# Three edits to the hand-ordered stages of a hybrid streaming layer: the place of the sink column, the engine of the weight splits, and the prices by which the order is made

## The chip, the cores and the metric

The kernel runs on one core of a Trainium2 chip. The metric is the device time of one execution in microseconds (us). The kernel before takes 1554.15 us, the median of three runs that lie between 1549.72 and 1560.18 us.

The engines of the core are named as the profile names them: PE is TensorE (matmuls and transposes; PEld is its weight load), DVE is VectorE, ACT is ScalarE, POOL is GpSimd, SP is SyncE, which only issues DMAs here. Each engine works through its own queue in the order in which the instructions were written.

## The reference, cut to what matters

One layer for 2048 prompt tokens and 32 sample tokens (2080 columns), model width 1024, in float32:

```
h = rmsnorm(x);  z = h @ W_in        # split into q, k, v, gate_a, B, C, u, gate_c, merge_a, merge_c
q, k = rope(rmsnorm(q)), rope(rmsnorm(k))                # 8 q heads, 2 kv heads, head_dim 64
# attention: each chunk of 64 frames sees itself and the two chunks before it
m = maximum(max(s), sink);  e = exp(s - m);  p = e / (sum(e) + exp(sink - m))
y_a = ((p @ v) * silu(gate_a)) @ W_attn_out
y_c = (B * conv3(C * u) * silu(gate_c)) @ W_conv_out
r   = x + (sigmoid(merge_a) * y_a + sigmoid(merge_c) * y_c) @ W_o
out = r + sigmoid(r @ W_ple_gate) * (p_in @ W_ple_proj)
```

The learned sink of a head is one more score in each row of the softmax, with no value behind it.

## The kernel before, in words

**Precision.** A float32 operand is made into two parts: a high part, rounded by a copy on ACT, and a low part, which is the operand less the high part, by one subtraction. A product is then three matmuls: high by high, high by low, low by high. So each weight tile of 128x512 costs a copy on ACT and a subtraction, and each row of activations does too.

**Stages.** Large matrix products are made in Strassen's way with seven products of half size (numbers 1 to 7 in the code). The program has three stages.

1. A first phase (lines 842 to 1166): the rows of the first half of the tokens are normalised and split while PE fills the time with the small product with W_ple_proj (`product0`), and then runs the first products of `z` (`step0`, the first entries of the list `steps`). It ends at about 85 us.
2. The bulk of `z`, whose instructions are ordered by the framework, up to about 860 us. Its weight splits are lines 206 to 208, high part on ACT and low part on DVE. The change does not touch it.
3. From line 1225 on, the attention and all products after it: `yB` (W_conv_out), `pp` (W_ple_proj), `yA` (W_attn_out), and the products `b` of W_o and W_ple_gate in two passes (s=0 and s=1, over the first and the second half of the columns). It runs from about 860 us to the end. PE works through a fixed list of units (`run_units`, `run_big`), and the 17 attention tiles (`attention`) are begun at set amounts of PE work and dropped in between the matmuls of the units.

**What sets the order.** In stages 1 and 3 the order of the instructions on every engine is written by a small plan that runs while the kernel is built. Each engine call goes through `Engine.__getattr__` (line 119), which adds the price of the instruction (`cost`, line 101) to the clock of its engine: `now` for PE, `busy["V"]` for DVE, `busy["S"]` for ACT, `busy["G"]` for POOL, `busy["Y"]` for SP. Pieces of work are Python generators. `yield {}` means: go on once what I issued has ended by the plan, and 0.15 us for the semaphore have passed; `yield {"ps": 2}` also waits until two PSUM banks are free. After each matmul `due()` issues whatever the plan says is ready. So a price decides in which place of an engine's queue an instruction stands. On the chip the instructions then wait on semaphores, each engine in that order. All such instructions have line 136 in the profile (`return f(**kw)`), so they are told apart by the names of their tiles.

**Prices before.** A DVE operation of n elements per partition costs 0.13 + 0.0011 n us (0.3 for 16 or fewer), an ACT operation 0.2 + 0.00082 n, a POOL operation 0.35 + 0.0021 n, and its end is where the engine's clock then stands.

**The weight splits of stage 3** (`split_w`, line 1884). A weight tile `wr` is loaded by SP; ACT writes the high part into `w`; the low part is made by POOL for all tiles of the list before the first one of the second pass (`last_split`, line 1895), and by DVE from there on. Five `w` tiles exist.

**Attention of one chunk** (`sink_attention`, line 1230). For each of two kv heads a PSUM bank `S` is taken. ACT first copies the sink into one more column of the bank (line 1235), then PE writes the scores, two matmuls (KH and KL) for each of two groups (lines 1238 and 1239). DVE takes the row maximum `nm` over scores and sink; ACT makes `E` = exp with its sum; DVE inverts the sum `se`; ACT scales into `P`; PE transposes into `PT`; ACT and DVE split it into `pth` and `ptl`; PE multiplies with V into `O`; DVE multiplies with the gate into `at`. Before that, `attention` transposes, normalises and rotates q and k; `qs`, `KH` and `KL` are the split operands of the scores, written by ACT (high) and DVE (low). For `ss` POOL raises to the power -0.5.

Tiles named below: `xb_h`, `xb_l` are split rows of the products `b`; `c` are their results; `tk`, `tb` rows of the merge gates; `acf`, `ac_l` rows of the gated attention; `kn`, `qr` normalised heads.

Of the kernel before, what the change touches and what calls it, by code (L numbers as in the profile page):

```python
# [7 lines left out]
F32 = mybir.dt.float32  # L8
# [34 lines left out]
def tile_hybrid_stream_step(ctx: ExitStack, tc: tile.TileContext, x, xT, pT, wu, consts, rope, ckT, cv_dup,  # L43
                            ck_raw, cv_raw, yT, kpo, vpo, cpo, kso, vso, cso):
    nc = tc.nc
    add, sub, mul = ALU.add, ALU.subtract, ALU.mult
# [10 lines left out]
    def bank(name):  # L57
        return psp.tile([P, 512], F32, tag="ps", name=name)
# [28 lines left out]
    now, fin, seq, events = [0.0], [0.0], [0], []  # L87
    busy = {"V": 0.0, "S": 0.0, "G": 0.0, "Y": 0.0}
# [6 lines left out]
    def size(ap):  # L95
        n = 1
        for d in ap.shape[1:]:
            n *= d
        return n

    def cost(key, op, kw):
        if op == "dma_start":
            return 0.9 if kw.get("accum_op") is not None else 0.57 if key == "G" else 0.42
        n = size(kw["out"])
        if key == "T":
            return max(0.109, 0.00044 * n + 0.0064)
        if key == "S":
            return 0.2 + 0.00082 * n + (0.13 if kw.get("accum_out") is not None else 0.0)
        if key == "G":
            return 2.03 if kw.get("op") == ALU.pow else 0.35 + 0.0021 * n  # L110
        if op == "tensor_reduce":
            return 0.08 + 0.0012 * size(kw["in_"])
        return 0.3 if n <= 16 else 0.13 + 0.0011 * n

    class Engine:
        def __init__(self, key, engine):
# [2 lines left out]
        def __getattr__(self, op):  # L119
            f = getattr(self.engine, op)  # L120

            def call(**kw):
                us = cost(self.key, op, kw)
                if self.key == "T":
                    now[0] += us
                    end = now[0]
                else:
                    busy[self.key] = end = max(busy[self.key], now[0]) + us
                if op == "dma_start":
                    if wire[0] is None:  # L130
                        end += 6.6 if kw.get("accum_op") is not None else 5.2
                    else:
                        o = kw["out"]
                        wire[0] = end = max(end + 1.7, wire[0]) + o.shape[0] * size(o) * 4 / 390e3
                fin[0] = max(fin[0], end)
                return f(**kw)  # L136
            return call

    eV, eS, eG, eT, eY = [Engine(*x) for x in (("V", nc.vector), ("S", nc.scalar), ("G", nc.gpsimd), ("T", nc.tensor),
                                           ("Y", nc.sync))]  # L140
# [5 lines left out]
    def free(tag, n=1):  # L146
        live[tag] -= n
        assert live[tag] >= 0, tag
# [72 lines left out]
    G = len(groups)  # L221
# [78 lines left out]
    def tile_of(gs, q):  # L300
        return "AB GF DE C".split().index(next(x for x in "AB GF DE C".split() if q in x)) if len(gs) == 2 else q == "C"

    worder = []
    for s in steps:
        for s_ in s:
            key = ("s", *s_) if len(s_) == 3 else ("l", *s_[1:3], tile_of(s_[1], s_[3]))
            if key not in worder:
                worder.append(key)
    for kind, b, n, *p in plan:
        key = {"B": (kind, b, n, *p), "yB": ("q", 0, UY + n, 1), "pp": ("pp", b, n // 2),  # L310
               "yA": ("q", b, UY + n, 0)}[kind]
        key = ("pp", 2, n // 2) if kind == "pp" else key
# [181 lines left out]
    def norm(v, k, rb, q):  # L494
        nc.vector.scalar_tensor_tensor(out=v, in0=v, scalar=lng_sb[:, k:k + 1], in1=rb[:, :q], op0=mul, op1=mul)
# [8 lines left out]
    B, T = {}, {}  # L504
# [725 lines left out]
    def sink_attention(name, ng, lhs, krhs, cn, e_out, norm, keys, sk, done, last, lag):  # L1230
        GG = 2 * ng
        SS = []
        for kv in range(2):
            s = bank(f"S_{name}_{kv}").rearrange("p (g c) -> p g c", g=2)
            eS.copy(out=s[:, :ng, cn:cn + 1], in_=sk[:, kv * ng:(kv + 1) * ng].unsqueeze(2))
            kh, kl = krhs(kv)
            for j in range(ng):
                eT.matmul(out=s[:, j, :cn], lhsT=lhs(kv, j), rhs=kh, start=True, stop=False)
                eT.matmul(out=s[:, j, :cn], lhsT=lhs(kv, j), rhs=kl, start=False, stop=True)
            SS.append(s)  # L1240
        if last:
            free("qs")
        yield {}
        nmax = sm.tile([P, 4], F32, tag="nmax", name=f"nm_{name}")
        for kv in range(2):
            eV.tensor_reduce(out=nmax[:, kv * ng:(kv + 1) * ng], in_=SS[kv][:, :ng, :cn + 1],
                            axis=AX.X, op=ALU.max, negate=True)
        yield {}
        se = sm.tile([P, 4], F32, tag="se", name=f"se_{name}")
        for kv in range(2):  # L1250
            for j in range(ng):
                g = kv * ng + j
                eS.activation(out=e_out(kv, j), in_=SS[kv][:, j, :cn + 1], func=AF.Exp, bias=nmax[:, g:g + 1],
                              accum_out=se[:, g:g + 1])
            yield None
            yield None
        yield {}
        free("ps", 2)
        eV.reciprocal(out=se[:, :GG], in_=se[:, :GG])
        yield {}  # L1260
        for kv in range(2):
            for j in range(ng):
                g = kv * ng + j
                for src, dst in norm(kv, j):
                    eS.activation(out=dst, in_=src, func=AF.Copy, scale=se[:, g:g + 1])
            if kv == 0:
                yield None
        fin[0] += lag
        yield {"ps": 2, "ph": 1}
        w = ng * P  # L1270
        pts, parts = [], []
        for q0 in range(0, len(keys), 512 // w):
            qs = keys[q0:q0 + 512 // w]
            pp = bank(f"PT_{name}_{q0}")
            for i, (ins, kp_, vh, vl) in enumerate(qs):
                for j, src in enumerate(ins):
                    eT.transpose(out=pp[:kp_, i * w + j * P:i * w + (j + 1) * P], in_=src, identity=ident)
            cols = 256 if q0 else 512
            ph = sm.tile([P, cols], F32R, tag=f"pth{cols}", name=f"pth_{name}_{q0}", bufs=2)
            pl = sm.tile([P, cols], F32R, tag=f"ptl{cols}", name=f"ptl_{name}_{q0}", bufs=2)  # L1280
            i = 0
            while i < len(qs):
                e = i
                while e < len(qs) and qs[e][1] == qs[i][1]:
                    e += 1
                n = qs[i][1]
                parts.append((ph[:n, i * w:e * w], pl[:n, i * w:e * w], pp[:n, i * w:e * w]))
                i = e
            pts += [(ph[:n, i * w:(i + 1) * w], pl[:n, i * w:(i + 1) * w], vh[:n], vl[:n])
                    for i, (_, n, vh, vl) in enumerate(qs)]  # L1290
        yield {}
        free("P")
        for h, _, src in parts:
            eS.copy(out=h, in_=src)
        yield {}
        for x, (h, lo, src) in enumerate(parts):
            if x:
                yield None
            eV.tensor_tensor(out=lo, in0=src, in1=h.bitcast(F32), op=sub)
        yield {"ps": -1}  # L1300
        O = bank(f"O_{name}")
        for i, (ph, pl, vh, vl) in enumerate(pts):
            eT.matmul(out=O[:, :w], lhsT=vh, rhs=ph, start=(i == 0), stop=False)
            eT.matmul(out=O[:, :w], lhsT=vl, rhs=ph, start=False, stop=False)
            eT.matmul(out=O[:, :w], lhsT=vh, rhs=pl, start=False, stop=(i == len(pts) - 1))
        yield {}
        free("ph")
        done(O)
        yield {}
        free("ps")  # L1310
        if last:
            last()
# [571 lines left out]
    def split_w(i):  # L1884
        w = wp.tile([P, 2, 4, P], F32R, tag="w", name=f"w{i}")
        W2[i] = h, lo = w[:, 0], w[:, 1]
        src = raw_of.pop(i)
        eS.copy(out=h, in_=src)
        yield {}
        (eG if i < last_split else eV).tensor_tensor(out=lo, in0=src, in1=h.bitcast(F32), op=sub)  # L1890
        yield {}
        w_ready[i] = now[0]
        room["wf"] += 1

    last_split = next(i for i, key in enumerate(worder) if key[:2] == ("B", 1))
    x_at, load_at = [0], [0]
    LEAD, LOOK = 2, 11

    def next_loads():
# [33 lines left out]
        while n_split[0] < len(worder) and room["w"] > 0:  # L1933
            i = n_split[0]
            if landed.get(i, 1e9) > now[0] or busy["S"] >= now[0] + (0.3 if i > used[0] + 2 else 1.5):
                break
            room["w"] -= 1
            go(split_w(i))
            n_split[0] += 1
# [165 lines left out]
```

## Time and profile before

| | |
|---|---|
| runs of the kernel before | 1554.15 us median, 1549.72 to 1560.18 |
| the profiled execution | 1554.51 us, its span 1552.7 us |
| busy in the span: PE, DVE, ACT, POOL | 1504.6, 1219.8, 816.9, 491.6 us |
| mean granted PE clock | 0.990 |

The profile is of one execution. The 1.8 us between its own time and its span lie around the first and the last instruction. A row of "windows" gives a stretch from:to in us, its length, and then for PE, PEld, DVE, ACT and POOL the busy time with the number of instructions, the PE clock that was granted as a share of full speed, the share of DMA time, and GB/s. A row of "waits" reads: engine, tile and line that waited, the arrow, what ended the wait, then the total in us, the number of waits, and the longest. A row of the "timeline" is the start in us, the duration, engine, line, operation, out<-in, shape, how many of them in a row, and in brackets the idle time of the engine just before it with what ended it. A row of "groups" gives operation, tiles, shape and count, then total busy us and mean ns of one.

### The profile page before, as it was taken

What the parts mean: (1) busy time and instruction counts of PE and PEld (TensorE: products, weight loads), DVE (VectorE), ACT (ScalarE), POOL (GpSimd) and SP (SyncE); (2) the same over time, 40 slices, a digit from 0 to 9 for tenths busy, and PEclk for the clock granted to TensorE, in tenths of its full rate; (3) what the DMA queues carried; (4) which work ended last, traced back from release to release, by engine and by line L of the source; (5) the groups of instructions that cost most, each with busy time, mean ns of one, the idle gap of its engine ahead of it and who ended that gap; (6) DMA issues with size and microseconds to landing.
All of it is one profiled execution on the core that took longest, in us unless ns stands there. A gap on an engine that the chain in (4) does not pass through costs nothing. (4 is left out here: it accounts for less than half of the span.)

```text
span 1552.7 us, 28012 instructions
## 1 busy us (share of the span) xinstructions
PE 1504.6 (97%) x9553; PEld 1358.6 (87%) x9553; DVE 1219.8 (79%) x2242; ACT 816.9 (53%) x1933; POOL 491.6 (32%) x622
## 2 busy tenths in 40 slices
PE   9999999999999999999999999999988997999998
PEld 7878888888899999999999899887877886999998
DVE  7887878875689777899757678857799899569777
ACT  8453353344467544344556356775755676444453
POOL 2133322232212332344212222236647455410201
PEclk9999999999999999999999999999999999999999
DMA  9489886898778845344647766567847659995959
GB/s 336 156 295 341 312 301 211 270 348 274 248 255 276 284 160 159 118 135 133 196 162 251 246 221 202 185 184 222 195 122 197 155 170 270 256 266 143 256 146 279
DMA packets 199230, 346.88 MB, mean 223 GB/s; under 512 B 23728, under 2 KB 57072, under 8 KB 199088
## 3 DMA queue, kind: packets, MB, share of 16 engines
q1 hardware_dynamic: 157008, 239.42, 48.2%
q0 software_dynamic: 32432, 87.85, 19.8%
q10 hardware_dynamic: 9648, 17.83, 3.1%
q8 instruction: 75, 1.23, 0.3%
q14 instruction: 67, 0.55, 0.1%
HBM read 227.66 MB, written 117.46 MB: 222 GB/s over the span
## 5 line engine op out<-in xcount | busy, mean ns | idle before, releaser
L136 PE MATMUL b<-xb_h,w 128*128 128x264 f32 (+1 forms) x1344 | 314.2, 325 | 0.0
L136 PEld LDWEIGHTS b<-xb_h,w 128*128 128x128 f32 x1344 | 225.5, 190 | 19.0
L591 PE MATMUL a<-x_l,w 128*128 128x264 f32 (+1 forms) x744 | 228.1, 320 | 0.0
L589 PE MATMUL a<-x_h,w 128*128 128x264 f32 (+1 forms) x744 | 227.2, 320 | 0.1
L136 PE MATMUL b<-xb_l,w 128*128 128x264 f32 (+1 forms) x672 | 218.1, 325 | 0.0
L594 PE MATMUL a<-x_h,w 128*128 128x264 f32 (+1 forms) x744 | 201.5, 320 | 0.0
L207 ACT CAST w<-wr 128x512 fp32r<-128x512 f32 (+1 forms) x180 | 110.1, 618 | 105.2 <-PE c L594 34.5
L208 DVE TENSOR_TENSOR w<-wr,w 128x512 fp32r<-128x512 f32 (+1 forms) x180 | 136.6, 769 | 34.4 <-ACT w L207 34.0
L136 POOL TENSOR_TENSOR w<-wr,w 128x512 fp32r<-128x512 f32 x88 | 127.0, 1495 | 110.5 <-ACT w L136 96.1
L136 ACT CAST w<-wr 128x512 fp32r<-128x512 f32 x168 | 102.5, 620 | 106.1 <-PE b L136 31.5
L589 PEld LDWEIGHTS a<-x_h,w 128*128 128x128 f32 x744 | 139.9, 188 | 10.8 <-DVE s L795 0.3
L591 PEld LDWEIGHTS a<-x_l,w 128*128 128x128 f32 x744 | 139.7, 188 | 10.7
L136 PEld LDWEIGHTS b<-xb_l,w 128*128 128x128 f32 x672 | 127.8, 190 | 9.5
L594 PEld LDWEIGHTS a<-x_h,w 128*128 128x128 f32 x744 | 125.0, 188 | 10.5
L727 PE MATMUL la<-x_h,w 128*128 128x264 f32 x516 | 111.7, 285 | 1.2 <-ACT w L207 1.2
L589 PE MATMUL c<-x_h,w 128*128 128x512 f32 (+1 forms) x336 | 110.6, 340 | 0.0
L591 PE MATMUL c<-x_l,w 128*128 128x512 f32 (+1 forms) x336 | 110.7, 339 | 0.0
L207 ACT CAST w<-a 128x512 fp32r<-128x512 f32 x82 | 49.7, 621 | 98.2 <-DVE a L338 31.8
L594 PE MATMUL c<-x_h,w 128*128 128x512 f32 (+1 forms) x336 | 100.4, 340 | 0.0
L788 DVE SCALAR_TENSOR_TENSOR u<-u,c 128x264 f32<-128x264 f32 (+1 forms) x125 | 59.4, 507 | 44.8 <-ACT u L783 29.8
L136 PE MATMUL yB<-ycs_h,w 128*128 128x264 f32 (+1 forms) x384 | 91.0, 326 | 0.0
L136 PE MATMUL yA<-ac_h,w 128*128 128x264 f32 (+1 forms) x384 | 90.5, 325 | 0.0
(436 smaller groups left out, 3949.0 us busy)
## 6 DMA issues: line engine op xcount, KB each, us to landing
wr<-in_wu SPq DMA_DIRECT2D x177, 256.0 KB, 4.0
a<-in_wu SPq DMA_DIRECT2D x116, 256.0 KB, 5.2
wr<-ws SPq DMA_DIRECT2D x74, 256.0 KB, 3.5
wr<-qs SPq DMA_DIRECT2D x64, 256.0 KB, 4.1
ws<-a POOLq DMA_DIRECT2D x63, 256.0 KB, 4.0
qs<-a POOLq DMA_DIRECT2D x24, 256.0 KB, 5.7
z_s<-s2n POOLq DMA_DIRECT2D x21, 264.0 KB, 4.2
s<-z_s SPq DMA_DIRECT2D x21, 264.0 KB, 5.0
```

Of the source, the lines that this page charges most:

```text
L136: return f(**kw)
L207: nc.scalar.copy(out=hi, in_=src)
L208: nc.vector.tensor_tensor(out=lo, in0=src, in1=hi.bitcast(F32), op=sub)
L589: nc.tensor.matmul(out=ps[:, :cn], lhsT=w[:, 0, k], rhs=x[0][:, c0:c0 + cn], start=first and k == 0, stop=False, skip_group_check=True)
L591: nc.tensor.matmul(out=ps[:, :cn], lhsT=w[:, 0, k], rhs=x[1][:, c0:c0 + cn], start=False, stop=False, skip_group_check=True)
L594: nc.tensor.matmul(out=ps[:, :cn], lhsT=w[:, 1, k], rhs=x[0][:, c0:c0 + cn], start=False, stop=k == 3, skip_group_check=True)
L727: nc.tensor.matmul(out=ps[:, :m], lhsT=w[:, a, k], rhs=r[:, cols], start=q in "ABG" and j == 0 and e == 0, stop=j == 1 and e == 2, skip_gr ...
L788: nc.vector.scalar_tensor_tensor(out=t[:, c0:c0 + cn], in0=t[:, c0:c0 + cn], scalar=-1.0, in1=ps[:, :cn], op0=mul, op1=sub)
```

## The change

There are three edits.

- The prices of `cost` are set anew. A DVE operation costs 0.045 + 0.0011 n (0.09 for 16 or fewer), an ACT operation 0.1 + 0.00082 n, reductions 0.01 + 0.0012 n. A new table `LATE` is added to the end of an operation, though not to its engine's clock: so the time from one instruction to the next on an engine (the pitch) and the time at which a result is there are told apart. A POOL operation that is not a DMA now also moves DVE's clock, by 0.35 of its price (`BESIDE`). PE's prices move by about 1%. Both hand-ordered stages use these prices, so also the first steps of the first phase.
- In `sink_attention` the copy of the sink column stands after the score matmuls of both banks, with a `yield {}` between them, and another before the maximum.
- In `split_w` all low parts are made by DVE; `last_split` is gone.

No DMA, no matmul and no arithmetic is added or taken away. The diff in full:

```diff
--- before.py
+++ after.py
@@ -98,19 +98,22 @@
             n *= d
         return n
 
+    LATE = {"V": 0.08, "S": 0.1, "G": 0.25, "Y": 0.0}
+    BESIDE = [0.35]
+
     def cost(key, op, kw):
         if op == "dma_start":
-            return 0.9 if kw.get("accum_op") is not None else 0.57 if key == "G" else 0.42
+            return 0.6 if key == "G" else 0.42
         n = size(kw["out"])
         if key == "T":
-            return max(0.109, 0.00044 * n + 0.0064)
+            return max(0.1085, 0.000446 * n + 0.0028)
         if key == "S":
-            return 0.2 + 0.00082 * n + (0.13 if kw.get("accum_out") is not None else 0.0)
+            return 0.1 + 0.00082 * n + (0.13 if kw.get("accum_out") is not None else 0.0)
         if key == "G":
             return 2.03 if kw.get("op") == ALU.pow else 0.35 + 0.0021 * n
         if op == "tensor_reduce":
-            return 0.08 + 0.0012 * size(kw["in_"])
-        return 0.3 if n <= 16 else 0.13 + 0.0011 * n
+            return 0.01 + 0.0012 * size(kw["in_"])
+        return 0.09 if n <= 16 else 0.045 + 0.0011 * n
 
     class Engine:
         def __init__(self, key, engine):
@@ -125,7 +128,10 @@
                     now[0] += us
                     end = now[0]
                 else:
-                    busy[self.key] = end = max(busy[self.key], now[0]) + us
+                    busy[self.key] = max(busy[self.key], now[0]) + us
+                    end = busy[self.key] + LATE[self.key]
+                    if self.key == "G" and op != "dma_start":
+                        busy["V"] = max(busy["V"], now[0]) + BESIDE[0] * us
                 if op == "dma_start":
                     if wire[0] is None:
                         end += 6.6 if kw.get("accum_op") is not None else 5.2
@@ -1232,7 +1238,6 @@
         SS = []
         for kv in range(2):
             s = bank(f"S_{name}_{kv}").rearrange("p (g c) -> p g c", g=2)
-            eS.copy(out=s[:, :ng, cn:cn + 1], in_=sk[:, kv * ng:(kv + 1) * ng].unsqueeze(2))
             kh, kl = krhs(kv)
             for j in range(ng):
                 eT.matmul(out=s[:, j, :cn], lhsT=lhs(kv, j), rhs=kh, start=True, stop=False)
@@ -1240,6 +1245,9 @@
             SS.append(s)
         if last:
             free("qs")
+        yield {}
+        for kv in range(2):
+            eS.copy(out=SS[kv][:, :ng, cn:cn + 1], in_=sk[:, kv * ng:(kv + 1) * ng].unsqueeze(2))
         yield {}
         nmax = sm.tile([P, 4], F32, tag="nmax", name=f"nm_{name}")
         for kv in range(2):
@@ -1887,12 +1895,11 @@
         src = raw_of.pop(i)
         eS.copy(out=h, in_=src)
         yield {}
-        (eG if i < last_split else eV).tensor_tensor(out=lo, in0=src, in1=h.bitcast(F32), op=sub)
+        eV.tensor_tensor(out=lo, in0=src, in1=h.bitcast(F32), op=sub)
         yield {}
         w_ready[i] = now[0]
         room["wf"] += 1
 
-    last_split = next(i for i, key in enumerate(worder) if key[:2] == ("B", 1))
     x_at, load_at = [0], [0]
     LEAD, LOOK = 2, 11
 
```

## The prediction, as put on record before the changed kernel was run

> **What bounds the kernel now.** I read the page first, then the busy time by stretch, then who PE waits for, then single stretches of the timeline.
>
> ```profile
> span 1552.7 us, 28012 instructions
> ```
>
> The profiled execution took 1554.51 us, 1.8 more than this span, and lies 0.4 above the median of the runs shown, so sums made against it hold for the median too. By stretch:
>
> ```profile
> 0.00:85.00 85.00, 81.71 (x350) 64.71 (x351) 68.89 (x116) 53.05 (x96) 18.49 (x38) 1.00 0.67 243
> 85.00:860.00 775.00, 771.73 (x4903) 699.82 (x4902) 606.81 (x1118) 368.60 (x757) 224.31 (x363) 1.00 0.70 236
> 860.00:1100.00 240.00, 226.06 (x1485) 204.84 (x1485) 170.10 (x359) 147.97 (x480) 79.62 (x69) 0.98 0.69 210
> 1100.00:1325.00 225.00, 203.79 (x1033) 169.61 (x1033) 206.45 (x337) 145.50 (x409) 124.22 (x105) 0.96 0.70 185
> ```
>
> PE is the bound up to 860 us: in the first phase it is idle for 3.3 of 85 us, and there is nothing more to be had there. The loss is in the third stage: 14 us idle from 860 to 1100, 21 us from 1100 to 1325. In the latter DVE is busy for 206 of 225 us, more than PE. The waits of PE in these two stretches:
>
> ```profile
> PE S L136 <- ACT S L136: 6.0, 6, 2.5
> PE S L136 <- DVE kn L136: 3.8, 1, 3.8
> PE pq L136 <- DMA zq<-z_q: 3.0, 1, 3.0
> ```
>
> ```profile
> PE S L136 <- ACT S L136: 12.4, 5, 5.8
> PE O L136 <- DVE ptl L136: 8.7, 3, 5.1
> ```
>
> Nearly all of it is one kind: score matmuls that wait for ACT's copy of the sink into their bank. The largest shows why. PE first, then ACT, then DVE:
>
> ```profile
> 1130.22 0.40 PE L136 MATMUL b<-xb_l,w 128*128 128x512 f32 x1
> 1136.46 0.53 PE L136 MATMUL S<-KH,qs 128*128 128x192 f32 x1 [5.84 <-ACT S L136]
> ```
>
> ```profile
> 1134.71 0.59 ACT L136 COPY c<-b 128x512 f32<-128x512 f32 x1
> 1135.19 1.15 ACT L136 ACTIVATE xb_h<-tk 128x512 fp32r<-128x512 f32 x2
> 1136.24 0.24 ACT L136 COPY S<-cst 128x2 f32<-128x2 f32 x2
> ```
>
> ```profile
> 1131.51 0.69 DVE L136 TENSOR_TENSOR qs<-pqt,qs 64x512 fp32r<-64x512 f32 x1
> ```
>
> The two copies take 0.24 us, but they stand in ACT's queue behind work that waits for DVE. PE starts as they end, while the last operand, `qs`, had been there since 1132.20. The 3.8 us put down to `kn` are of this kind in my reading, since only the sink copies, the operands of the scores and the bank stand before an `S` matmul, and `kn` feeds none of these at that point.
>
> The PE clock adds to each long wait. Five stretches behind a wait were run at half the clock (the first two, and the sum of all five):
>
> ```profile
> 1011.90:1015.30 3.40, 3.37 (x15) 3.37 (x16) 3.20 (x7) 0.88 (x4) 0.00 (x0) 0.50 0.16 48
> 1080.10:1083.60 3.50, 3.50 (x14) 3.11 (x14) 1.31 (x4) 1.29 (x3) 0.91 (x2) 0.51 0.67 210
> ...
> sum 27.30, PE 24.13 PEld 21.52 DVE 20.42 ACT 14.02 POOL 10.90; mean PE 4.83 PEld 4.30 DVE 4.08 ACT 2.80 POOL 2.18
> ```
>
> PE was busy for 24.1 us in them, so 12.1 us were lost; 3.4 of these before 1100 (half of 3.37 and 3.50), 8.6 after.
>
> The second cause is POOL. Its weight splits hold up DVE:
>
> ```profile
> 1308.42 4.08 POOL L136 TENSOR_TENSOR w<-wr,w 128x512 fp32r<-128x512 f32 x3
> 1308.54 5.78 DVE L136 SCALAR_TENSOR_TENSOR ac_l<-acf,ac_h 128x528 fp32r<-128x528 f32 x1
> ```
>
> One DVE operation stands for 5.8 us beside three splits in a row. In groups, from 1100 to 1325, with a later stretch without splits on POOL behind it:
>
> ```profile
> L136 DVE TENSOR_TENSOR xb_l<-c,xb_h 128x512 fp32r<-128x512 f32 x28 | 29.1, 1054 | 2.4 <-ACT xb_h L136 2.2
> L136 DVE TENSOR_TENSOR c<-c,b 128x512 f32<-128x512 f32 x33 | 22.2, 676 | 3.0 <-PE b L136 1.5 <-ACT c L136 1.4
> L136 DVE SCALAR_TENSOR_TENSOR xb_l<-tk,xb_h 128x512 fp32r<-128x512 f32 x20 | 18.4, 940 | 0.1
> ...
> L136 DVE SCALAR_TENSOR_TENSOR c<-c,c 128x512 f32<-128x512 f32 x12 | 12.5, 1045 | 0.1
> L136 DVE SCALAR_TENSOR_TENSOR c<-c,pp 128x512 f32<-128x512 f32 x13 | 11.0, 853 | 0.1
> ...
> L136 DVE TENSOR_TENSOR qr<-tt 128x256 f32<-128x256 f32 x12 | 7.9, 657 | 0.0
> L136 DVE SCALAR_TENSOR_TENSOR ac_l<-acf,ac_h 128x528 fp32r<-128x528 f32 x4 | 7.9, 1970 | 0.0
> ...
> L136 DVE TENSOR_TENSOR kn<-tt 128x64 f32<-128x64 f32 x12 | 6.9, 572 | 0.0
> ```
>
> ```profile
> L136 DVE TENSOR_TENSOR w<-wr,w 128x512 fp32r<-128x512 f32 x52 | 35.5, 687 | 9.4 <-ACT w L136 9.0 <-DMA pp<-z_pp 0.2
> L136 DVE SCALAR_TENSOR_TENSOR xb_l<-tk,xb_h 128x528 fp32r<-128x528 f32 x28 | 19.0, 700 | 0.2 <-ACT xb_h L136 0.2
> ```
>
> Operations of 512 elements that take 0.69 to 0.70 us later take 0.85 to 1.05 here, `ac_l` 1.97, while `c<-c,b`, which reads PSUM, takes its 0.68 in the same stretch.
>
> **The change part by part.**
>
> *The sink column.* No instruction is added; the 64 copies move from before to behind the score matmuls. What is late next for those matmuls is `qs`: in the wait shown, 1.6 of 5.8 us stay (1132.20 against PE's idle from 1130.62), and I let the same 27% stay of all. From 860 to 1100 this frees 73% of 9.8 us, 7.2; from 1100 to 1325, 73% of 12.4, 9.1. On the other side, the maximum now waits for the two copies and one more turn of the plan, about 0.5 us per chunk (0.24 for the copies and the plan's 0.15 us for a semaphore), with two banks held as long. The cover is PE's fixed list of units: no wait of PE in the rows above is for the end of a chunk. Without it 31 chunks would pay some 15 us. ACT may stand for PE's scores at these copies, with weight copies queued behind; it has 80 idle us in the 225, so I take nothing for it.
>
> *The splits on DVE.* POOL's splits in the critical stretch:
>
> ```profile
> L136 POOL TENSOR_TENSOR w<-wr,w 128x512 fp32r<-128x512 f32 x54 | 78.6, 1524 | 51.5 <-ACT w L136 49.5 <-DMA pp<-z_pp 1.6 <-DMA zq<-z_q 0.3
> ```
>
> For 54 of them DVE has to pay. One costs its queue not 0.69 us but the time until the next can start:
>
> ```profile
> 1197.58 0.68 DVE L136 TENSOR_TENSOR c<-c,b 128x512 f32<-128x512 f32 x1
> 1198.17 0.22 DVE L136 TENSOR_TENSOR kn<-tt 128x64 f32<-128x64 f32 x1
> 1198.31 0.42 DVE L136 TENSOR_TENSOR qr<-tt 128x256 f32<-128x256 f32 x1
> ```
>
> From 1197.58 to 1198.17 are 0.59; I take 0.60, so +32.4 us. What DVE gets back, by the groups above against 0.687 for 512 elements, 0.700 for 528, and 0.22 and 0.42 for `kn` and `qr`: 28 × 0.367 = 10.3; 20 × 0.253 = 5.1; 12 × 0.358 = 4.3; 13 × 0.166 = 2.2; 12 × 0.237 = 2.8; 4 × 1.27 = 5.1; 12 × 0.352 = 4.2; together 34.0. So DVE's need in this stretch goes from 206.5 to 204.9: the move costs DVE nothing, and it takes the long stops out. With them go the waits of `O` for `ptl`; of 8.7 I take 8. POOL's queue loses 79 us of work that its DMA issues and the `ss` powers stood behind; no wait of PE is for these, so I count nothing.
>
> *Does DVE let PE have it?* Without the waits PE would need 203.8 − 8.6 (clock) + what stays of its waits (21.2 − 9.1 − 8 = 4.1) = 199.3 us for this stretch. DVE needs 204.9 and is never packed full; the best 50 us of the stretch are
>
> ```profile
> 1250.00:1300.00 50.00, 46.41 (x248) 38.60 (x247) 48.68 (x81) 35.07 (x102) 29.09 (x24) 1.00 0.75 208
> ```
>
> 97.4%, so 204.9 becomes 210.4. DVE is then the bound, and the stretch falls by 14.6 us rather than 25.7.
>
> [...] If each of the 54 splits stopped DVE for its whole 1.52 us, DVE would win back up to 79 us, not 34, and be no bound; the first rival below gives the time.
>
> *The prices.* They change no instruction, only places in queues. New prices for 512 elements are 0.608 (DVE) against 0.59 measured above, so the plan will know DVE's load in the tight stretch. In the first phase 3.3 us at most can be won. Bounds: PE starts that wait about 0.1 us more for each of some 40 splits, +4, and −2. I take 0: DVE and ACT are busy there for 69 and 53 of 85 us.
>
> *Sum.* 860 to 1100: 7.2 + 3.4 = 10.6. 1100 to 1325: 14.6. After 1325 the splits are on DVE already, save six; nothing. 1554.5 − 25.2 = **1529.3 us**.
>
> **The rivals.**
>
> *DVE is no bound* (chance 0.22). If DVE wins back more than the seven groups show, its need falls under PE's 199.3 us, and the stretch falls by 25.7: 1554.5 − 10.6 − 25.7 = 1518.2. For it: the 5.8 us stop shows that a DVE operation can lose more than the 4.1 us beside it. Against it: the mean excess, 34 us over 54 splits, is 0.6 us each.
>
> *DVE takes all of it back* (0.20). The freed time comes back as waits of `O`, `S` and `PT` for DVE, and 1100 to 1325 stays at 225: 1554.5 − 10.6 = 1543.9. For it: 206 of 225 busy now, and prices without slack put operations closer together. Against it: long stops, not the mean load, end PE's waits today.
>
> *DVE over its capacity* (0.08), the other side. If DVE's long operations have another cause than POOL, nothing comes back: 206.5 + 32.4 = 238.9 us, 13.9 over the stretch, 1554.5 + 13.9 − 10.6 = 1557.8; with DVE packed as loosely as now (206.5 of 225) it is 260, and 1579. I take 1568. It decides as soon as DVE wins back less than 14 of the 32 us. Against it: the rows without POOL's splits beside them.
>
> *The order does not do what it says*: if the `S` waits are really for `qs`, only the DVE part acts. That the operands stood ready 4 us before PE began speaks against it; it is part of the 0.20.
>
> **How the numbers follow.** The forecast's own case (1521 to 1538) has 0.47, and the rest, 0.03, is a first phase that loses 4 us or more. The range holds the low rival with 6 us for the `S` waits that I let stay, 1512, and reaches over the 1544 case to the place where DVE just fails to win, 1553. Under 1% no measurement here tells a difference; 1% is 1538.6 and 1569.7. Faster: 0.47 + 0.22 + half of the 0.03, 0.71. Slower by over 1%: about half of the 0.08 and a rest, 0.06. Same: 0.23.
>
> **What would show it.** Right: no wait of PE `S` for ACT `S`; all weight splits of the third stage on DVE and none on POOL; `xb_l<-c` 128x512 near 0.69 us; DVE over 95% busy where PE now loses 21 us; at most two half-clock stretches. The first phase keeps its 3.3 us. It is wrong if PE waits for `nm`, `PT` or `ptl` for more than 12 us in all, if `xb_l` stays over 0.9 us, or if the time before 860 us changes by more than 4 us.

## The result, and the profile after

The changed kernel takes 1534.84 us (median of 4 runs, 1533.54 to 1536.18) against 1552.41 for the kernel before on the same chips: a ratio of 0.9879, 95% interval 0.9841 to 0.9917. Forecast were 1529.3 us and a range from 1512 to 1553. The profiled execution took 1534.6 us with a span of 1532.8.

The two executions are compared by places in PE's list of work, since a time in us means another place in each. The marks are the first matmul of `yB` (the third stage begins), the last run of `b` before the attention rows of the second half come in, and the first `yA` after that. Windows of the kernel before:

```profile
855.30:1121.30 266.00, 252.06 (x1633) 227.21 (x1632) 192.24 (x406) 165.43 (x525) 94.29 (x81) 0.98 0.71 211
1121.30:1332.80 211.50, 190.29 (x951) 157.82 (x950) 191.78 (x308) 135.92 (x381) 114.90 (x97) 0.95 0.69 185
1332.80:1552.70 219.90, 213.49 (x1753) 213.28 (x1751) 164.76 (x309) 95.94 (x180) 41.16 (x46) 1.00 0.82 223
```

The same work in the changed kernel:

```profile
861.30:1118.30 257.00, 249.81 (x1641) 226.28 (x1640) 204.65 (x444) 166.20 (x526) 49.12 (x47) 0.99 0.73 218
1118.30:1312.50 194.20, 182.84 (x935) 151.29 (x934) 183.01 (x352) 133.10 (x366) 47.17 (x48) 0.98 0.71 194
1312.50:1532.80 220.30, 214.34 (x1759) 214.09 (x1757) 168.47 (x314) 99.39 (x193) 34.55 (x40) 1.00 0.82 229
```

The third stage went from 697.4 to 671.5 us, 25.9 less: 9.0 before the tight stretch, 17.3 in it, nothing behind it. But the stage begins 6.0 us later, at 861.3 instead of 855.3. These two numbers are the result: a gain of 26 and a loss of 6, and 20 less in all between the two profiled executions; between the medians of the runs it is 17.6.

The waits of PE after:

```profile
PE pq L142 <- DMA zq<-z_q: 4.9, 1, 4.9
PE b L142 <- DVE c L142: 4.4, 3, 3.3
PE PT_s L142 <- ACT Ps L142: 3.2, 1, 3.2
PE b L142 <- ACT xb_h L142: 2.7, 1, 2.7
PE pr L142 <- DVE sq L142: 1.9, 1, 1.9
```

No `S` waits for ACT any more, and no `O` for `ptl`. DVE from 1100 to 1310 us, in groups:

```profile
L142 DVE TENSOR_TENSOR w<-wr,w 128x512 fp32r<-128x512 f32 x56 | 39.4, 709 | 0.3
L142 DVE TENSOR_TENSOR c<-c,b 128x512 f32<-128x512 f32 x35 | 23.8, 680 | 4.4 <-PE b L142 3.4 <-ACT c L142 0.8
L142 DVE TENSOR_TENSOR xb_l<-c,xb_h 128x512 fp32r<-128x512 f32 x28 | 18.6, 682 | 3.0 <-ACT xb_h L142 2.9
L142 DVE SCALAR_TENSOR_TENSOR xb_l<-tk,xb_h 128x512 fp32r<-128x512 f32 x20 | 13.8, 715 | 0.6 <-ACT xb_h L142 0.5
```

`xb_l<-c` fell from 1.05 to 0.68 us, and weight splits came in: 56 in this window, 50 of them between the marks of the tight stretch, where POOL had 49 before. Still DVE is busy there for 183.0 us where it had 191.8, with all but a few of the other operations the same. The half-clock stretches of PE after:

```profile
16.20:23.00 6.80, 6.80 (x20) 5.54 (x20) 3.72 (x9) 4.40 (x9) 3.28 (x5) 0.50 1.04 405
886.60:893.40 6.80, 4.76 (x22) 4.76 (x23) 2.63 (x6) 2.19 (x5) 0.73 (x1) 0.50 1.05 372
1132.30:1135.70 3.40, 3.40 (x11) 2.73 (x11) 3.33 (x10) 3.40 (x12) 0.00 (x0) 0.50 0.52 77
1214.20:1217.60 3.40, 3.31 (x9) 2.60 (x9) 3.28 (x10) 1.59 (x4) 0.68 (x1) 0.51 0.02 5
```

Three are left in the third stage where there were six stretches of 30.7 us in all (the five that the prediction counts and one from 882.2, 3.4 us long), and one is new, in the first phase.

### The profile page after: what moved, and what is told of

Read it like the earlier page. It is cut to its first block, busy times and chain, and to the rows that moved or that the text cites. A ratio compares the mean times of both kernels' runs of the same rounds, so it can differ in the third digit from the quotient of the medians.

```text
span 1532.8 us, 27951 instructions
## 1 busy us (share of the span) xinstructions
PE 1499.9 (98%) x9553; PEld 1355.6 (88%) x9553; DVE 1226.7 (80%) x2330; ACT 818.1 (53%) x1933; POOL 374.0 (24%) x534
## 3 DMA queue, kind: packets, MB, share of 16 engines
q0 software_dynamic: 32432, 87.85, 19.9%
## 4 chain that ended last, share of the span: by engine, by line
PE 85%; DVE 6%; ACT 4%; DMA 3%; issue 1%; SPq 0%; ACTq 0%; DVEq 0%
PE b L142 18%; PE a L595 7%; PE a L600 7%; PE a L597 7%; PE la L733 5%; PE yA L142 5%; PE yB L142 5%; PE c L597 4%; PE c L600 4%; PE c L595 4%; PE lc L733 2%; PE pp L142 2%; PE O L142 2%; PE S L142 2%; DVE c L142 1%
## 5 line engine op out<-in xcount | busy, mean ns | idle before, releaser
L214 DVE TENSOR_TENSOR w<-wr,w 128x512 fp32r<-128x512 f32 (+1 forms) x180 | 133.1, 749 | 36.7 <-ACT w L213 35.0
L142 DVE TENSOR_TENSOR w<-wr,w 128x512 fp32r<-128x512 f32 x168 | 118.0, 707 | 15.0 <-ACT w L142 13.9
L794 DVE SCALAR_TENSOR_TENSOR u<-u,c 128x264 f32<-128x264 f32 (+1 forms) x125 | 59.5, 507 | 39.4 <-ACT u L789 28.2
```

Source lines behind the costliest of these rows:

```text
L214: nc.vector.tensor_tensor(out=lo, in0=src, in1=hi.bitcast(F32), op=sub)
L794: nc.vector.scalar_tensor_tensor(out=t[:, c0:c0 + cn], in0=t[:, c0:c0 + cn], scalar=-1.0, in1=ps[:, :cn], op0=mul, op1=sub)
```

## The experiments

Theory after the result: the three edits gave the third stage's 26 us, the sink column and the splits most of it, and the new prices cost 6 us in the first phase. Rivals: the prices gave the 26 us, and the 6 us are chance.

**One edit, or two, at the old prices, and the first phase.** `e_sink` is the kernel before with the second edit of the diff alone, `e_split` with the third alone, `e_two` with both. `e_first` is the changed kernel with the old prices up to the end of the first phase; `cost0` there is the old `cost`, and `...` stands for lines left out:

```diff
+    PITCH = [False]
     def cost(key, op, kw):
+        if not PITCH[0]:
+            return cost0(key, op, kw)
...
-                    end = busy[self.key] + LATE[self.key]
-                    if self.key == "G" and op != "dma_start":
+                    end = busy[self.key] + (LATE[self.key] if PITCH[0] else 0.0)
+                    if PITCH[0] and self.key == "G" and op != "dma_start":
...
     def restart():
+        PITCH[0] = True
```

Expected of `e_sink`: 

> The kernel before with the sink edit alone (old prices, POOL keeps its splits). Theory: the 18 us of S waits for ACT go, but the long DVE operations stay (xb_l 128x512 near 1.0 us), so the O waits stay and some S wait comes back for qs: about 1541 us, 8 to 15 under the kernel before. Rival (the order by pitch made the gain of the third stage): within 4 us of the kernel before.

Measured: 1550.22 us, ratio 0.9970 (in brackets, here and below, the 95% interval: 0.9957 to 0.9984), 4.9 us less. That is under the theory's 8 to 15 and nearly the rival's 4.

Expected of `e_split`: 

> The kernel before with the weight splits on DVE alone (old prices, sink column first). Theory: xb_l 128x512 falls from 1.05 to 0.69 us, the O waits (8.7 us) go and the S waits for ACT shrink, since ACT stands less behind DVE: about 1540 us. Rival (DVE is the bound, the splits only load it): no faster than the kernel before, 1554 or more.

Measured: 1566.48 us, ratio 1.0068 (1.0044 to 1.0093), 11.3 us more. The theory missed. The waits of PE in it:

```profile
PE S L136 <- ACT S L136: 12.1, 6, 3.2
PE b L136 <- DVE w L136: 9.0, 3, 4.2
```

Expected of `e_two`: 

> Sink edit and splits on DVE, at the old prices. Theory: the first two stages keep the time of the kernel before (855 us to the first yB), the third gains about 20 of the 26 us that the changed kernel gained: 1532 us, no slower than the changed kernel. Rival (prices): under half of the gain of the third stage, 1543 us or more.

Measured: 1549.33 us, ratio 0.9965 (0.9950 to 0.9979), 5.8 us less, which is on the rival's side. The `S` waits for ACT are gone, and PE waits for DVE instead:

```profile
PE b L136 <- DVE xb_l L136: 7.1, 3, 4.3
PE b L136 <- DVE w L136: 3.8, 2, 2.0
PE b L136 <- DVE c L136: 3.6, 2, 2.4
```

Expected of `e_first`: 

> The changed kernel with the old prices in the first phase only. Theory: the new order of the first phase cost the 6 us that came before the first yB (861.3 against 855.3), and the third stage is untouched: 1529 us. Rival (the 6 us are chance, such as the phase of the clock's half-speed stretch): 1533 to 1536 us, like the changed kernel.

Measured: 1529.20 us, ratio 0.9825 (0.9803 to 0.9847), 26.0 us less than the kernel before. So the sink column and the splits together are worth 6 us at the old prices and the prices 20 more in the third stage. My account of the gain had fallen, though its sum was near.

**The new prices in the third stage, with one edit or none.** All three have the old prices in the first phase, as `e_first`. New theory: the edits need each other. `e3_p` has neither edit, `e3_sp` has the sink column behind the scores, `e3_dp` has the splits on DVE. `e_z2` is `e_first` with two loads of `zq` allowed at once:

```diff
-    limit = {... "z": 1, "ga": 2, ...}
+    limit = {... "z": 2, "ga": 2, ...}
```

Expected of `e3_p`: 

> The kernel before with the new prices in the third stage alone: sink column first, first-pass splits on POOL. After the first runs the account is: sink and splits together gave 6 us at the old prices, so the prices give the rest, about 20. Theory now (the edits need each other): with POOL still stopping DVE and the sink copies still ahead, prices alone give under 10, 1545 or more. Rival (the prices make the gain by themselves): 1535 us or less.

Measured: 1567.01 us, ratio 1.0075 (1.0048 to 1.0102), 15.2 us more. The rival falls, and the sign was not what the theory had either: the prices alone make the kernel slower. PE waits 17 times for the sink where it did 11 times:

```profile
PE S L160 <- ACT S L160: 19.6, 17, 3.0
```

Expected of `e3_sp`: 

> New prices in the third stage and the sink edit; first-pass splits stay on POOL. Theory (POOL's splits stop DVE and no price can place that): long DVE operations stay (xb_l 128x512 near 1.0 us), PE waits for DVE of 8 us and more, 1538 us. Rival (the plan's 0.35 share of POOL's time on DVE covers it): within 3 us of the version with all three, 1529 to 1532.

Measured: 1538.15 us, ratio 0.9896 (0.9875 to 0.9917), 13.7 us less: as the theory had it. The largest of PE's waits in all is the one for `ptl` again, and the long DVE operations are there:

```profile
PE O L160 <- DVE ptl L160: 6.9, 2, 3.5
```

```profile
L160 DVE TENSOR_TENSOR xb_l<-c,xb_h 128x512 fp32r<-128x512 f32 x28 | 25.6, 926 | 0.5 <-ACT xb_h L160 0.4
```

Expected of `e3_dp`: 

> New prices in the third stage and splits on DVE; sink column first as in the kernel before. Theory: S waits for ACT of 8 to 15 us and two or three half-clock stretches come back, 1542 us. Rival (exact prices put the sink copy in time, so its place does not matter): 1529 to 1532.

Measured: 1546.08 us, ratio 0.9959 (0.9940 to 0.9977), 5.8 us less, 4 us slower than the theory had it, and with more waits than its 8 to 15 us:

```profile
PE S L160 <- ACT S L160: 17.0, 12, 2.9
```

Expected of `e_z2`: 

> All three edits with the old prices in the first phase, and two query tiles of attention (limit z 2 for 1) on their way at once, to take away the 4.3 us wait of PE pq for the load of zq and the half-clock stretch behind it. Theory: the load is issued one tile earlier and the wait goes, 1523 to 1526 against 1529. Rival (the load waits on the DMA queue, not on the limit): 1529.

Measured: 1528.22 us, ratio 0.9834 (0.9808 to 0.9860): no better than `e_first`. PE still waits 3.4 us for `zq`. The limit is not what makes that load late; what does is open.

**DVE's capacity, POOL's work beside it, and the first phase again.** `e_double` and `e_pool` are `e_first` with these lines in `split_w`, the first for `e_double`, the second for `e_pool` (behind the split on DVE), where `idle_t` is a tile of 128x128 that nothing else uses and `last_split` is as in the kernel before:

```diff
-        eV.tensor_tensor(out=lo, in0=src, in1=h.bitcast(F32), op=sub)
+        for _ in range(2 if i < last_split else 1):
+            eV.tensor_tensor(out=lo, in0=src, in1=h.bitcast(F32), op=sub)
```

```diff
+        if i < last_split:
+            for _ in range(3):
+                nc.gpsimd.tensor_tensor(out=idle_t, in0=idle_t, in1=idle_t, op=sub)
```

Expected of `e_double`: 

> All three edits, old prices in the first phase; the low part of each first-pass weight tile is made twice by DVE, the same numbers into the same place (88 more DVE operations of about 0.60 us, 53 us in all, some 50 of them where DVE is busy for 183 of 194 us). Theory (DVE is the bound of that stretch): about 30 us more there against 11 us of idle time, so 20 to 30 us more, 1549 to 1559. Rival (the stretch is limited by order and latency, with DVE to spare): under 8 us more, 1537 or less.

Measured: 1582.15 us, ratio 1.0179 (1.0156 to 1.0202), 53 us more than `e_first`, which took 1529.03 on the same chip when it was run again (`e_first2`). The theory's side, but twice its 20 to 30 us. The windows of the tight stretch and of the `yA` and `b` units behind it, first `e_double`, then `e_first2`:

```profile
1112.70:1334.90 222.20, 189.60 (x897) 153.82 (x895) 212.91 (x388) 124.27 (x326) 41.33 (x42) 0.90 0.64 164
1334.90:1427.10 92.20, 82.26 (x629) 79.67 (x628) 66.21 (x129) 44.94 (x117) 18.40 (x22) 0.94 0.86 232
```

```profile
1113.00:1307.00 194.00, 182.93 (x935) 151.19 (x934) 182.74 (x352) 132.94 (x366) 47.84 (x48) 0.98 0.72 196
1307.00:1375.00 68.00, 68.00 (x560) 67.97 (x559) 48.29 (x90) 30.71 (x66) 12.96 (x15) 1.00 0.96 271
```

The tight stretch grew by 28.2 us while DVE's busy time in it grew by 30.2; the stretch behind it grew by another 24.2, with more matmuls in it (629 for 560), attention that had slipped, and with waits and half clock that `e_first2` does not have there. A doubled split also makes its weight tile later, but of that PE feels little; its large waits are for DVE's other work:

```profile
PE b L160 <- DVE c L160: 7.6, 1, 7.6
PE pk L160 <- DVE kr L160: 7.0, 1, 7.0
PE b L160 <- DVE w L160: 1.8, 1, 1.8
```

So DVE has nothing to spare in the tight stretch. 88 operations at 0.60 are 53 us, and 53 came out; that the two agree is chance, since only 28 of the 53 us lie where DVE is full.

Expected of `e_pool`: 

> All three edits, old prices in the first phase; POOL does three idle subtractions of 128x128 in a tile of its own with each first-pass weight tile, which nothing waits for and the plan does not price (the work done is that of the reference, plus these). Theory (POOL stops DVE): DVE operations with two SBUF inputs get long again (xb_l 128x512 at 0.85 to 1.0 us), 15 to 25 us more, 1544 to 1554. Rival (POOL's splits cost by their own latency of 1.5 us, not by stopping DVE): under 4 us more, xb_l at 0.68.

Measured: 1544.19 us, ratio 0.9942 (0.9923 to 0.9962), 15.2 us more than `e_first`, at the lower end of the theory. The tight stretch, and one group of DVE from 1100 to 1310:

```profile
1114.60:1321.90 207.30, 187.84 (x935) 153.97 (x934) 197.62 (x355) 133.06 (x367) 132.03 (x197) 0.96 0.68 185
```

```profile
L160 DVE TENSOR_TENSOR xb_l<-c,xb_h 128x512 fp32r<-128x512 f32 x28 | 20.6, 754 | 2.7 <-ACT xb_h L160 2.6
```

With PE doing the same work (935 matmuls), and POOL doing work that nobody waits for, DVE's busy time rises from 182.7 to 197.6 us and the stretch from 194.0 to 207.3. `xb_l` rises to 0.75 only, not to the 0.85 expected. The idle work also stands before POOL's own DMA issues and `ss` powers, but PE has no wait for POOL among its waits, and the idle time before DVE's costliest groups was ended by ACT and PE.

Expected of `e_after2`: 

> The changed kernel again, beside the next one on the same chip. Theory: 1535 us, and its first yB some 5 us later than with the old order of the first phase. Rival (its lag is chance): 1530 us.

Measured: 1534.33 us, ratio 0.9881 (0.9859 to 0.9903).

Expected of `e_first2`: 

> All three edits with the old prices in the first phase again, beside the changed kernel on the same chip. Theory: 1529 us, 5 to 6 under the changed kernel. Rival: equal within 2 us.

Measured: 1529.03 us, ratio 0.9837 (0.9814 to 0.9859), 5.3 under the changed kernel on the same chip. The stages up to the first `yB`, in the changed kernel and then in `e_first2`, divided at the first `a` of the second stage:

```profile
0.00:149.20 149.20, 145.12 (x611) 116.45 (x612) 118.46 (x195) 79.86 (x143) 40.99 (x79) 0.98 0.78 272
149.20:861.30 712.10, 707.81 (x4614) 647.46 (x4613) 552.06 (x1029) 339.59 (x705) 202.16 (x321) 1.00 0.68 227
```

```profile
0.00:147.35 147.35, 144.51 (x610) 115.49 (x611) 117.70 (x195) 80.16 (x144) 40.08 (x78) 0.99 0.77 274
147.35:856.20 708.85, 705.70 (x4614) 646.58 (x4613) 552.40 (x1030) 339.13 (x705) 200.67 (x321) 1.00 0.69 229
```

The first `yB` came at 861.3 and 863.9 us in the two profiles of the new order, and between 854.0 and 857.2 in the kernel before and all the other experiments, which have the old order. So there is a lag that is not chance; its size is 4 to 10 us by these places and 5.3 by the runs.

## Why the prediction came out as it did, point by point

**The sum and its account.** The third stage was forecast to fall by 25.2 us and fell by 25.9; before the tight stretch 10.6 were forecast and 9.0 came, in it 14.6 and 17.3, behind it 0 and 0. That the sum came so near is luck, because the account of who gives it was wrong. I had put all of it on the sink column and the splits and wrote of the prices that "they change no instruction, only places in queues". What these versions gained or lost, each with the old order of the first phase and against the kernel before on the same chip (times of the whole program):

| edits in the third stage | old prices | new prices |
|---|---|---|
| none | 0 | +15.2 |
| sink column | −4.9 | −13.7 |
| splits on DVE | +11.3 | −5.8 |
| both | −5.8 | −26.0 |

As the last edit, each is worth 12 to 20 us: the splits 12.3, the sink column and the prices 20.2. Alone, two of the three cost time. The step that failed is the price step, where I weighed the first phase only and gave the third stage nothing. There the prices are worth 20.2 of the 26.0 us once the other two edits are in, and these two give 5.8 without them: the waits that I saw end by two edits come back in other places (`b` for DVE in `e_two`) as long as the order is made for the wrong durations. Why the prices need the other two I can only argue: the new ones leave no slack, so what the plan cannot see, a POOL split that makes DVE's operations long (`xb_l` 1.05 us against 0.68) or a sink copy held in ACT's queue, reaches PE at once. Nor was it tried which of the new prices does it: the shorter DVE and ACT prices, `LATE`, `BESIDE` or the DMA price.

All nine versions fit one reckoning. Take from the length of the third stage PE's idle time up to its last matmul and half of PE's busy time at half clock, and 647 to 652 us are left, the work itself and some 6 us after the last matmul: 697.4 − 35.1 − 13.8 = 648.5 before, 671.6 − 18.6 − 5.8 = 647.2 after, 709.4 − 41.4 − 19.9 = 648.1 in `e_split`, 711.8 − 44.1 − 16.2 = 651.5 in `e3_p`. So every gain and loss in the table is waits of PE and the clock behind them, as the first part of the prediction read it (it missed one of the six half-clock stretches, 1.7 us).

**The sink column.** Right as a cause: with the copies ahead of the scores, `S` waits for ACT are 12.1 to 19.6 us in every version, and with the copies behind them there is none. Alone it gives 4.9 us; with the splits on DVE 17, with the new prices 29, with both 20.

**The splits on DVE.** The need of DVE was forecast to stay (206.5 to 204.9 us from 1100 to 1325); between the marks, over nearly the same work, it fell from 191.8 to 183.0, so DVE won back more than the seven groups showed. That POOL's splits are what makes DVE's operations long is shown twice: `xb_l<-c` takes 1.05 us in the kernel before and 0.93 in `e3_sp`, which have them on POOL, 0.68 in the changed kernel and in `e_first`, which have them on DVE, and 0.75 beside POOL work that nothing waits for (`e_pool`).

**DVE as the bound.** Borne out by `e_double`: 30.2 us more of DVE's work made the tight stretch 28.2 us longer. DVE is busy for 183.0 of 194.2 us, 94.2%, not the 97.4% I took; the smaller need made up for it. PE is busy there for just as long, 182.8 us, so the two are level, and its idle time went from 21.2 to 11.4 us.

**The first phase.** "I take 0", with bounds −2 and +4: it was +6.0, outside the bounds, and it is nearly the whole difference of 5.5 us between forecast and result. It is the case to which I gave 0.03, "a first phase that loses 4 us or more". By the profile, 3.5 of them came before the first `a` of the second stage (149.2 against 145.7): 6.8 us at half clock, where PE was busy throughout, are 3.4, behind a wait of 1.9 us for `sq`. The second profile of this order has waits of 2.0 and 2.0 there and one half-clock stretch of 3.4. One such stretch, from 17.9 us, is also in `e_first2`, which has the old order, and none in the kernel before, so part of the 3.4 us is how the clock fell. The other 2.5 us lie in the second stage (712.1 against 709.6), whose instructions the diff does not touch; its waits grew by 1.1 us in all, and the rest I can't name. Which of the new prices does it was not tried.

**What was to show it.** No `S` wait for ACT, no split on POOL, `xb_l` at 0.68: as said. Three half-clock stretches in the third stage instead of two, and DVE at 94% instead of over 95%. "The first phase keeps its 3.3 us" was wrong, and one of my own signs of being wrong came: the time before 860 us changed by more than 4. The rivals: DVE taking all of it back and DVE over its capacity did not come. "DVE is no bound" had its condition, since DVE won back more than the seven groups show, but not its time: the stretch fell by 17.3 us, not 25.7. `e_split`, 11 us slower, is not a case of DVE over its capacity: DVE was busy for 199 of 225 us there between 1100 and 1325.

The best version is `e_first`: all three edits, with the old prices in the first phase, 1529.03 and 1529.20 us.

## What to carry to other kernels

Where the order of queues is written by a plan, price, placement and engine are one edit: here two of three made it slower by themselves, and judging them one at a time would have thrown away 20 us. I would price with the pitch only what the plan can see whole, and first take out of the queues what it can't see, such as one engine making another's operations longer, here `xb_l` from 0.68 to 1.05 us; that this is the reason is argued, not shown. And look at each stage that shares the prices: the one with nothing to win has only something to lose.

## What the runs showed of the hardware

In the clock records of both profiles the half-clock stretches up to PE's last matmul last 3.413 or 6.827 us and begin whole steps of 3.413 us apart: those above, at 16.2, 886.6, 1132.3 and 1214.2 us, by 255, 72 and 24 steps, and the six of the kernel before by 38, 20, 16, 20 and 34. A wait of 2 to 3 us cost nothing more in one place and 1.7 us in another: PE idled 2.46 us before 1079.17 in the kernel before and ran at half clock from 1080.1, and idled 2.61 us before 1309.99 with full clock behind it. So the clock did not add to "each long wait", as the prediction has it. By whole steps back from the stretches at 1080.1 and 1319.1, the first wait lies within one step, in which PE was busy for 0.98 us; the second has a border between two steps, 1308.8, in its middle, and PE was busy for 1.95 and 2.26 us in these two. In the step before each of the ten stretches PE was busy for 0 to 1.61 us, but one step of 1.57 us, from 1275.7 in the changed kernel, has full clock behind it.

How much longer DVE's operations get is not told by POOL's busy time alone: 52 splits of 128x512, busy for 79.4 us, made `xb_l` 0.24 us longer on average in `e3_sp`, 153 operations of 128x128 and 0.62 us, busy for 94.8, only 0.07 in `e_pool`. Whether it is their size or the moment at which they run was not tried. `c<-c,b`, which reads PSUM, took 0.68 us in both.
